# Swapping the packet sizes of two slabs between load and store in a 90-degree rotation

## Chip, cores and metric

The kernel runs on one core of one Trainium2 chip. The metric is the device time of one execution in microseconds (us), lower is better. Engines: DVE is VectorE, ACT is ScalarE, SP is SyncE, which here issues all transfers. The 16 DMA engines serve one queue.

## The reference

```python
def setup_inputs():
    batch, c, h, w = 32, 3, 256, 256
    return {"x": np.random.randn(batch, c, h, w).astype(np.float32)}

def reference(x):
    return np.rot90(x, k=-1, axes=(-2, -1)).astype(np.float32)
```

96 images of 256 x 256 floats are turned. Nothing is computed: 25.17 MB are read and 25.17 MB written.

## The kernel before

The images are cut into 12 slabs of 2 MB, numbered 0 to 11, and all 12 fit into SBUF at once. Every slab is loaded, turned by transposes on DVE, and stored. A row of the result is a column of the source, so each slab has one of two layouts on the way in and the other, or for pairs of slabs the same, on the way out:

- "short": a partition holds 8 image rows, one contiguous run and so one packet of 8 KB, for each half of the slab. One transfer of all 128 partitions for both halves (two for slab 0, one for each half).
- "long": a partition holds 16 image rows, one packet of 16 KB. Two transfers of 64 partitions each, on the even and on the odd ones.

```python
    RL, RS = 16, 8
    I = 2
    ...
    long_st = (0, 1, 2)          # loaded short, stored long
    both = (8, 10)
    paired = [n + a for n in both for a in range(2)]   # loaded long, stored long
    ...
    for n in (0, 1, 2, 3, 7, 4, 5, 6, *range(8, n_slabs)):
        if n in (1, 2):
            nc.sync.dma_start(out=fours(units[n]), in_=ld_short[n])
            continue
        for i in range(I):
            if n in long_st:
                ld = nc.sync.dma_start(out=fours(units[n])[:, i], in_=ld_short[n][:, i])
            else:
                ld = nc.sync.dma_start(out=units[n][i::I], in_=ld_long[n, i])
            if (n, i) == (last, 0):
                mark = ld

    home = [turned0] + units[:last]      # slab n is turned into the place of slab n - 1
    ...
    def store(n):
        if n in paired:
            ...
        elif n in long_st:
            for i in range(I):
                nc.sync.dma_start(out=st_long[n, i], in_=home[n][i::I])
        else:
            return nc.sync.dma_start(out=st_short[n], in_=fours(home[n]))

    for n in range(both[0]):
        turn(n)
    for n in (4, 3, 5, 6, 7, 1, 2):
        st = store(n)
        if n == 4:
            tc.add_manual_dep(st.ins, mark.ins.name, ...)   # stores after loads
    for n in range(both[0], n_slabs):
        turn(n)
        store(n)
    ...
    store(0)
```

`mark` makes the first store wait until the last load but one has landed. So all loads come first and all stores after them, in one queue that does not run empty.

## Time and profile before

| | before |
|---|---|
| device time, median of three runs | 123.28 us (123.15 to 123.40) |
| span of the profiled run | 121.5 us |
| bytes moved, packets of the queue | 50.33 MB, 97.9% of 16 engines' span |
| DVE busy | 90.6 us |
| loads done, stores done (last data packet) | 61.64 us, 120.30 us |

The page of the profile gives totals and the span in 40 slices. The view by stretches gives, for each stretch of time: its length, the busy time of DVE, ACT and POOL, the clock, the mean busy share of the 16 DMA engines, and GB/s. The trace also holds a record of every packet (start, duration, size); means and ends of packets in this text are from those. "Loads done" is where the records have moved half of the bytes. The lines themselves stand in the prediction.

### The profile page before, as it was taken

Reading aid. Unit: us, or ns where it says so; the run is one execution under the profiler, and the core shown is the slowest. Engines: PE = TensorE matmul, PEld = TensorE weight load, DVE = VectorE, ACT = ScalarE, POOL = GpSimd, SP = SyncE. Lnnn points to the kernel's source line nnn. Section 1 sums busy time; section 2 is a strip of 40 time slices with the busy share of each in tenths; the row PEclk is TensorE's granted clock in tenths of the full one; section 3 lists DMA queues with packets and bytes.
Section 4 is the critical chain, followed back from the end, with each engine's and each line's share of the span. In section 5 each row is a group of like instructions: output and inputs, shape, how many; then the busy total and the mean of one; then the engine's idle time right before and its main releaser. Section 6 shows DMA issues by size and latency. Waiting matters only on the chain.

```text
span 121.5 us, 134 instructions
## 1 busy us (share of the span) xinstructions
DVE 90.6 (75%) x24; ACT 4.9 (4%) x3; POOL 0.2 (0%) x4
## 2 busy tenths in 40 slices
DVE  0029999999999999999999999999999960000000
ACT  0000000000000000000040000000000038000000
POOL 0000000000000000000000000000000000000000
DMA  3999999999999999999999999999999999999994
GB/s 73 426 429 426 432 458 426 426 421 421 432 432 432 421 432 432 426 426 432 432 405 426 421 429 431 432 423 431 453 432 432 432 432 432 432 432 432 432 432 173
DMA packets 4752, 50.33 MB, mean 414 GB/s; under 512 B 656, under 2 KB 656, under 8 KB 656
## 3 DMA queue, kind: packets, MB, share of 16 engines
q1 hardware_dynamic: 4752, 50.33, 97.9%
HBM read 25.17 MB, written 25.17 MB: 414 GB/s over the span
## 4 chain that ended last, share of the span: by engine, by line
DVE 59%; issue 13%; DMA 6%; DVEq 3%; ACT 2%; ACTq 1%; SPq 0%
DVE u L116 53%; DVE turned L116 6%; DMA u<-in_x_dram 6%; DVEq L169 3%; ACT u L141 2%; ACTq L169 1%; SPq L92 0%; DVEq L116 0%
## 5 line engine op out<-in xcount | busy, mean ns | idle before, releaser
L116 DVE STREAM_TRANSPOSE u<-u 128x2048 f32<-128x2048 f32 x22 | 83.5, 3866 | 0.3
L116 DVE STREAM_TRANSPOSE turned<-u 128x2048 f32<-128x2048 f32 x2 | 7.1, 3586 | 8.2 <-DMA u<-in_x_dram 8.2
L141 ACT COPY u<-turned 128x2048 f32<-128x2048 f32 x2 | 3.6, 1869 | 35.6 <-DVE u L116 35.6
L141 ACT ACT_TABLE_LOAD x1 | 1.3, 1283 | 62.2 <-DMA u<-in_x_dram 62.2
L158 POOL MEMSET const-bfloat16-1.0<- 128x1 bf16 x1 | 0.1, 101 | 0.0
L158 POOL MEMSET const-uint8-127<- 128x1 uint8 x1 | 0.1, 101 | 0.0
L158 POOL MEMSET const-float32-0.0<- 128x1 f32 x1 | 0.1, 98 | 0.2 <-issue 0.2
L158 POOL MEMSET const-float32-1.0<- 128x1 f32 x1 | 0.1, 98 | 0.0
## 6 DMA issues: line engine op xcount, KB each, us to landing
u<-in_x_dram SPq DMA_DIRECT2D x20, 1024.0 KB, 19.6
out_dram<-u SPq DMA_DIRECT2D x14, 1024.0 KB, 15.6
out_dram<-u SPq DMA_DIRECT2D x5, 2048.0 KB, 16.0
u<-in_x_dram SPq DMA_DIRECT2D x2, 2048.0 KB, 13.7
```

The source lines that it names most:

```text
L116: nc.vector.transpose(out=dst[:, h * step : (h + 1) * step], in_=src[:, h * step : (h + 1) * step])
L141: nc.scalar.copy(out=fours(units[last])[:, i], in_=fours(turned0)[:, i])
L158: nc = _bacc.Bacc("TRN2", target_bir_lowering=False, num_devices=1)
L169: with _tile.TileContext(nc) as tc:
```

## The change

Slabs 1 and 2 change sides: loaded long (16 KB packets), stored short (8 KB packets). Their stores keep their place in the queue, behind those of slabs 4, 3, 5, 6 and 7, so that the stores of 8 KB packets lie together. The intent, as far as the edit shows it, is to load all but slab 0 with the larger packets.

```diff
-    long_st = (0, 1, 2)
+    long_st = (0,)
@@
-        if n in (1, 2):
+        if n in ():
             nc.sync.dma_start(out=fours(units[n]), in_=ld_short[n])
             continue
```

## The prediction

> **What bounds the kernel now.** I began with the page, for the total of the transfers. A kernel that only turns images by 90 degrees reads 25.17 MB and writes 25.17 MB, so the first question is whether the DMA engines ever rest.
>
> ```profile
> span 121.5 us, 134 instructions
> DVE 90.6 (75%) x24; ACT 4.9 (4%) x3; POOL 0.2 (0%) x4
> DMA  3999999999999999999999999999999999999994
> DMA packets 4752, 50.33 MB, mean 414 GB/s; under 512 B 656, under 2 KB 656, under 8 KB 656
> ...
> q1 hardware_dynamic: 4752, 50.33, 97.9%
> ```
>
> The DMA row is full from the second slice to the last but one, and the packets of the one queue fill 97.9% of 16 engines' span: 0.979 x 121.5 = 118.95 us of the 121.5. VectorE (DVE) has 90.6 us of work. The page's chain of waits nevertheless runs mostly through DVE:
>
> ```profile
> DVE 59%; issue 13%; DMA 6%; DVEq 3%; ACT 2%; ACTq 1%; SPq 0%
> DVE u L116 53%; DVE turned L116 6%; DMA u<-in_x_dram 6%; DVEq L169 3%; ACT u L141 2%; ACTq L169 1%; SPq L92 0%; DVEq L116 0%
> ```
>
> I do not take that chain for the bound. It follows instructions back and ends about 103 us into the span; after that only packets queued earlier drain, which no instruction stands for. The view by stretches decides. Its columns are the stretch in us, its length, busy time of DVE, ACT and POOL, clock, the mean busy share of the 16 DMA engines, and GB/s:
>
> ```profile
> 0.00:2.00 2.00, 0.00 (x0) 0.00 (x0) 0.20 (x4) 1.00 0.14 33
> 2.00:4.00 2.00, 0.00 (x0) 0.00 (x0) 0.00 (x0) 1.00 0.80 274
> 5.00:17.00 12.00, 8.74 (x3) 0.00 (x0) 0.00 (x0) 1.00 1.01 427
> 20.00:58.00 38.00, 37.83 (x10) 0.00 (x0) 0.00 (x0) 1.00 1.01 429
> 64.00:84.00 20.00, 19.97 (x6) 0.00 (x0) 0.00 (x0) 1.00 1.01 429
> 88.00:118.00 30.00, 11.13 (x4) 3.63 (x2) 0.00 (x0) 1.00 1.01 429
> ```
>
> I chose the four long stretches by kind of transfer: loads in 8 KB packets (slabs 0, 1, 2), loads in 16 KB packets (the rest), stores in 8 KB packets (slabs 4, 3, 5, 6, 7), stores in 16 KB packets (slabs 1, 2, 8 to 11, 0). All four move 427 to 429 GB/s with every engine busy. So the program is one queue of 50.33 MB: at 429 GB/s that is 117.3 us, plus the start (2.00 x 0.86 + 2.00 x 0.20 = 2.1 us lost in the first 4 us) and about 1.5 us after the last packet, 120.9 of the 121.5 us. The measured time, 123.28 us, is 1.8 us above the span, and I carry that over unchanged.
>
> **What the Trainium skill says.** "DMA: Bandwidth & Descriptors", section "Why small descriptors are slow (HBM only)", gives each packet a fixed overhead of about 3 cycles inside the engine, beside one cycle for every 32 bytes. For 8 KB that is 3 in 259 (1.2%), for 16 KB 3 in 515 (0.6%), so doubling the packet should save about 0.6% of a transfer. The trace agrees. Over the same four stretches its packet records have means of 310.0 ns (8 KB load), 614.1 ns (16 KB load), 309.0 ns (8 KB store) and 613.7 ns (16 KB store): two 8 KB packets cost 618 to 620 ns where one of 16 KB costs 614, 0.7 to 1%, the same in both directions. "SBUF — State Buffer", section "Door 1: The DMA port swizzle", warns that partitions 0 to 63 alone reach half of the ports; the 16 KB transfers here have 64 partitions too, but every second one of all 128, and their 429 GB/s shows that nothing is lost. The same page, "Who interferes with whom", says that transfers do not contend with the compute engines; the trace agrees: 429 GB/s with DVE fully busy (64 to 84 us) and also over 88 to 118 us, where it works 11 of 30 us.
>
> **The change part by part.** It moves slabs 1 and 2 from one group to the other.
> 1. Loads. Two issues of 2 MB, 512 packets of 8 KB, become four issues of 1 MB, 256 packets of 16 KB. Engine time 512 x 310.0 - 256 x 614.1 = 1.5 us less, over 16 engines 0.09 us less.
> 2. Stores. Four issues of 1 MB, 256 packets of 16 KB, become two of 2 MB, 512 packets of 8 KB. 512 x 309.0 - 256 x 613.7 = 1.1 us more, over 16 engines 0.07 us more.
> 3. Completion packets. There are 656 = 16 x 41 of them, for 41 transfers. Loads go from 22 to 24 and stores from 19 to 17: again 41, and 4096 data packets as before. Nothing gained or lost.
> 4. Sum on the path that sets the end: -0.02 us, that is, nothing. Each slab keeps one leg in each packet size; only the legs swap.
> 5. DVE. The order of instructions shows the same 24 transposes in the same order; four of them take the 16-rows-by-2 pattern in place of the 8-by-8 pattern with runs of 32 slots. The chain has the pair of slab 1 from 15.33 to 23.19 us (7.86), slab 2 to 31.03 (7.84), slab 3, which has the new pattern today, to 38.89 (7.86). No difference, and it lies beside the transfers anyway.
> 6. Arrival. DVE needs slab 1 at 15.33 and slab 2 at 23.19 us. In the records they land at 13.1 and 18.1 us. The bytes ahead of them in the queue stay the same, so they land within some tenths of that: 2 and 5 us of reserve.
> 7. Issue. SP keeps at most eight transfers open, since each waits for the one eight places before it. At the start those eight were 2 x 1 + 2 x 2 + 4 x 1 = 10 MB and become 8 MB, 20 us of work at 429 GB/s; the loads of 1 MB that run in this regime already take a median of 19.6 us from issue to landing with the engines at 1.01. In the stores the eight open ones now hold more bytes. Each 2 MB store is one issue of 0.4 to 0.9 us in place of two of about 1.4 us, so SP is free earlier, which is worth nothing while the queue is full.
>
> **Rivals.**
> - *The direction matters.* Writing to HBM in small packets could cost more than reading, so that the stores lose what the loads do not win back. For it: it is the only asymmetry in the change. Against it: 429 GB/s and 309 ns in 64 to 84 us, where exactly such stores run. Even 5% more on 4.19 MB (9.8 us) would be 0.5 us: 123.8.
> - *The queue runs dry at a hand-over.* The stores of slabs 8 and 9 wait for DVE at 84.73 us, those of 10 and 11 at 99.16. Against it: 14.7 MB of stores in front of slab 8 last from about 62 to 96 us, 11 us beyond its release; the 4.2 MB of slabs 8 and 9 then last to about 106, nearly 7 us beyond the second. One 2 MB store slot more or less in the ring of eight shifts what each issue waits for, but the slots waited for (stores of 3 to 7) are the oldest in the queue. A stall of one such transfer would cost at most 2 MB / 429 = 4.9 us: about 128.
> - *The start gets shorter.* Larger packets straight after slab 0 could fill the 16 engines sooner. Against it: slab 0 is still first in 8 KB packets, and its 16 packets on each engine cover the ramp, which is over by 4 us. At most some tenths: 123.0.
> - *DVE becomes the bound.* It would have to lose over 4 us (it ends at 99.2, the queue would be dry at about 106). Four instructions of unchanged length cannot do that.
>
> **Range and chances.** The sum leaves 123.28 - 0.02, so 123.26 us. Three runs of the kernel before spread from 123.15 to 123.4; the new one may also shift how the 16 engines finish relative to each other by up to half a 16 KB packet (0.3 us). I take 122.9 to 123.65. Two per cent are 2.5 us, over a hundred times the sum: faster by that 1%, slower by that 1% (only the dry queue would do it), the same 98%.
>
> **What would show it right or wrong.** Right: 4752 packets and 656 small ones again, about 98% of the queue's span, 427 to 429 GB/s in every stage, the first stretch now with 16 KB packets from about 8 us and the 8 KB stores lasting until about 96 us; mean transposes of 3.9 us; the first transpose still at 8.2 us. Wrong: a stretch of the DMA share below 0.95 between 4 and 118 us (a dry queue), a mean of 8 KB stores above 315 ns in 84 to 96 us (direction), or DVE waiting for a load at slab 1 or 2.

## The result, and the profile after

The changed kernel took 123.81 us in the median of six runs (123.68 to 124.01), against 123.30 us (123.15 to 123.40) for the kernel before. The ratio is 1.0044, 95% interval 1.0031 to 1.0057. A ratio here is the mean time of one kernel's fast runs over that of the other's of the same rounds, so it is not quite the ratio of the two medians. By the 2% rule that is "the same", but it is a real loss of half a microsecond, and it lies outside the predicted range.

The page of the changed kernel:

```profile
span 122.1 us, 134 instructions
DVE 90.4 (74%) x24; ACT 4.9 (4%) x3; POOL 0.2 (0%) x4
DMA  3999999999999999999999999999999999999993
DMA packets 4752, 50.33 MB, mean 412 GB/s; under 512 B 656, under 2 KB 656, under 8 KB 656
...
q1 hardware_dynamic: 4752, 50.33, 97.7%
...
DMA 51%; DVE 20%; issue 3%; DVEq 3%; SPq 3%; ACT 2%; ACTq 1%
```

Packets, bytes and the full DMA row are as predicted. The last line is the summary of the chain of waits. It now runs mainly over transfers where it ran over DVE before (59%), although neither kernel is bound by DVE: a reminder that this chain picks one of several ways that end close together.

The transposes, in the costliest groups (line, engine, operation, out and in, count, busy us, mean ns, idle before), of the kernel before:

```profile
L116 DVE STREAM_TRANSPOSE u<-u 128x2048 f32<-128x2048 f32 x22 | 83.5, 3866 | 0.3
```

and of the changed one:

```profile
L116 DVE STREAM_TRANSPOSE u<-u 128x2048 f32<-128x2048 f32 x22 | 83.4, 3848 | 0.3
```

DVE is not slower and waits no longer. The time must be in the queue. The view by stretches of the changed kernel, over the stretches of the prediction:

```profile
5.00:17.00 12.00, 8.80 (x3) 0.00 (x0) 0.00 (x0) 1.00 1.02 436
20.00:58.00 38.00, 37.83 (x10) 0.00 (x0) 0.00 (x0) 1.00 1.01 429
64.00:84.00 20.00, 19.96 (x6) 0.00 (x0) 0.00 (x0) 1.00 1.01 427
88.00:118.00 30.00, 10.91 (x4) 3.63 (x2) 0.00 (x0) 1.00 1.01 429
```

The early loads show 436 against 427 GB/s, the stretch of 8 KB stores 427 against 429. Both differences are too small to read from this view, which counts a packet whole where it starts: one 8 KB packet on each of 16 engines is 131 KB, which over 20 us is already 6.6 GB/s, and one 16 KB packet on each is 22 GB/s over 12 us. The very end tells more. The kernel before:

```profile
119.00:120.00 1.00, 0.00 (x0) 0.00 (x0) 0.00 (x0) 1.00 0.81 344
120.00:121.00 1.00, 0.00 (x0) 0.00 (x0) 0.00 (x0) 1.00 0.01 0
```

The changed one:

```profile
119.00:120.00 1.00, 0.00 (x0) 0.00 (x0) 0.00 (x0) 1.00 0.89 377
120.00:121.00 1.00, 0.00 (x0) 0.00 (x0) 0.00 (x0) 1.00 0.16 66
```

Before, all engines stop together shortly after 120 us. Afterwards some of them work on. The packet records give the sizes:

| | before | changed |
|---|---|---|
| first data packet starts | 1.76 us | 1.76 us |
| loads done | 61.64 us | 61.34 us |
| mean of 8 KB store packets, 63 to 76 us (slabs 4, 3, 5: not touched by the change) | 309.0 ns | 310.9 ns |
| share of those over 310 ns | 0% | 17% |
| mean of 8 KB store packets after 76 us | 309.1 ns | 311.8 ns |
| mean of 16 KB store packets after 99 us | 614.2 ns | 616.2 ns |
| mean end of the 16 engines' last packets | 120.21 us | 120.41 us |
| last of these ends | 120.30 us | 120.87 us |
| first to last of these ends | 0.14 us | 0.69 us |

"First to last" is called the end spread below. So the loads win 0.30 us, and the stores take 59.53 us where they took 58.66: 0.87 us lost. Of the net 0.57 us, 0.20 us is a later end in the mean over the engines, and 0.37 us is that the last engine ends further behind the mean. Stores are slow that are identical in both kernels.

The delay is not spread evenly. If each record is joined to the one whose end it meets, the queue falls into 16 strings of packets, presumably one for each engine (this joining is a reconstruction, not always unique; the records do not name the engine). A packet's record starts about 3 ns before the one ahead of it ends: 306 ns from start to start where each lasts 309, which is why the busy share can read 1.01. Durations in ns of consecutive 8 KB stores from 76 us on in the changed kernel, two strings of each sort, S being a completion packet:

```
S 309 309 309 309 309 309 309 309 309 309 309 309 309 309 309 309 S 309 309 309 ...
S 309 309 309 309 309 309 309 309 309 309 309 309 309 309 309 309 S 309 309 309 ...
S 315 318 313 314 316 316 312 313 319 312 313 314 314 316 312 314 S 318 316 312 ...
S 316 314 309 324 315 309 314 313 319 314 314 312 309 316 316 316 S 318 309 316 ...
```

Some strings run at exactly 309 ns for tens of microseconds, others have 309 to 324 ns and mostly over 310. The disturbance grows: in the changed kernel 11% of the 8 KB stores take over 310 ns from 63 to 66 us, 36% from 77 to 80, and 74% from 92 to 95. In the kernel before, every string between 63 and 66 us except for one packet reads 309 throughout.

### The profile page after: what moved, and what is told of

Its sections match the earlier page's. It is cut to its first block, busy times and chain, and to the rows that moved or that the text cites. A ratio compares the mean times of both kernels' runs of the same rounds, so it can differ in the third digit from the quotient of the medians.

```text
span 122.1 us, 134 instructions
## 1 busy us (share of the span) xinstructions
DVE 90.4 (74%) x24; ACT 4.9 (4%) x3; POOL 0.2 (0%) x4
## 4 chain that ended last, share of the span: by engine, by line
DMA 51%; DVE 20%; issue 3%; DVEq 3%; SPq 3%; ACT 2%; ACTq 1%
DMA u<-in_x_dram 45%; DVE u L116 20%; DMA out_dram<-u 6%; DVEq L169 3%; SPq L94 2%; ACT u L141 2%; ACTq L169 1%; SPq L92 1%; DVEq L116 0%; SPq L127 0%
```

## The experiments

Theory A: the changed loads leave the 16 engines in a relation to each other (their spacing in time) in which the stores then delay each other, changed or not. Theory B: the 8 KB stores of slabs 1 and 2 are what costs. Further rivals come up below: theory C is defined in the expectation of `split8`, D in that of `after_drain`, E in that of `before_nodve`. Each kernel ran beside the kernel before on the same chip; "8 KB stores" below is the mean of these packets from 63 to 76 us, which belong to slabs 4, 3 and 5, whose stores no experiment edits (from 64.5 us where the queue was emptied). These figures are of one profile for each run.

### The kernel before, again

No edit.

> The kernel before, unchanged, for a second profile and the noise of a run. All theories: ratio 1.000 within 0.001. If the spacing of the 16 engines in the queue is set by the program, the 8 KB stores between 64 and 84 us should again take a mean of 309.0 ns and the engines should finish the last transfer within 0.2 us of each other. If the spacing is a matter of luck in each run, this profile shows another spread.

123.32 us, ratio 1.0022 (0.9997 to 1.0046), not within the 0.001 expected: four of six runs took 123.16 to 123.32 us, but two took 123.99 and 124.03, longer than the median of the changed kernel. The profiled run is one of the four. In it the 8 KB stores had 309.5 ns and the end spread was 0.18 us, although the spread of the engines at the first landings was another one (0.71 us in place of 0.49). So that spread alone does not decide. But the program alone does not decide either: the kernel before can lose as much by itself. Of its other 55 runs none took over 123.65 us; no long run of it was profiled, so why two were long stays open.

### Only the loads

```diff
-        if n in (1, 2):
+        if n in ():
...
-            if n in long_st:
+            if n == 0:
                 ld = nc.sync.dma_start(out=fours(units[n])[:, i], in_=ld_short[n][:, i])
```

> Only the loads of slabs 1 and 2 take 16 KB packets; stores and transposes are those of the kernel before, so the result is wrong on purpose. Theory A (the loads set how the 16 engines are spaced in time, and that spacing later delays stores that the change never touched): the slowdown is here, 123.6 to 123.9 us, the unchanged 8 KB stores of slabs 4, 3, 5, 6, 7 at a mean above 310 ns, the last transfer finished over 0.5 us apart. Theory B (8 KB stores of slabs 1 and 2 are what costs): no slowdown, 123.0 to 123.3 us, 309.0 ns.

123.85 us, ratio 1.0045 (1.0033 to 1.0057): the whole loss. 8 KB stores 311.3 ns, 26% of them over 310, and the engines end 0.65 us apart. The result is wrong, as meant. Its last stretches:

```profile
119.00:120.00 1.00, 0.00 (x0) 0.00 (x0) 0.00 (x0) 1.00 0.88 377
120.00:121.00 1.00, 0.00 (x0) 0.00 (x0) 0.00 (x0) 1.00 0.12 49
```

Engines work past 120 us as in the changed kernel, although all its stores are those of the kernel before. This is the experiment that shows the cause as far as it is known: an edit of the loads alone slows stores that are the same.

### Only the stores

```diff
-        elif n in long_st:
+        elif n == 0:
             for i in range(I):
```

> Only the stores of slabs 1 and 2 take 8 KB packets; loads and transposes are those of the kernel before, so the result is wrong on purpose. Theory A: no slowdown, 123.2 to 123.4 us, 8 KB stores at 309.0 ns up to 96 us. Theory B: 123.6 to 123.9 us, with a mean above 311 ns between 84 and 96 us only.

123.43 us, ratio 1.0013 (1.0001 to 1.0025), end spread 0.20 us. 8 KB stores 309.0 ns up to 76 us, 309.9 ns after that, where the new ones lie. B is out as the cause of the half microsecond: these stores cost about 0.16 us, against 0.07 us predicted. Theory A's 123.2 to 123.4 us, with 309.0 ns throughout, was just missed too. The same two stretches:

```profile
119.00:120.00 1.00, 0.00 (x0) 0.00 (x0) 0.00 (x0) 1.00 1.23 524
120.00:121.00 1.00, 0.00 (x0) 0.00 (x0) 0.00 (x0) 1.00 0.01 0
```

### More transfers in the load queue, same packets

```diff
-        if n in (1, 2):
+        if n in ():
```

> The kernel before, with each 2 MB load of slabs 1 and 2 split into two of 1 MB, still in 8 KB packets; correct. Theory C (the number of transfers in the load queue, not the packet size, does it): 123.6 to 123.9 us. Theories A by packet size, and B: 123.2 to 123.4 us.

123.44 us, ratio 1.0012 (1.0000 to 1.0024), 8 KB stores 309.0 ns. The number of transfers (24 loads, as in the changed kernel) does not do it.

### Emptying the queue between loads and stores

Before and changed kernel, each with every store of the first loop waiting for the very last load:

```diff
-            if (n, i) == (last, 0):
+            if (n, i) == (last, I - 1):
...
-        st = store(n)
-        if n == 4:
+        for st in store(n):
             tc.add_manual_dep(st.ins, mark.ins.name, ...)
```

(`store` returns the list of its transfers for this.)

> The kernel before, but the first stores wait for the last load itself and not for the one before it, so that the queue runs empty at the hand-over and the 16 engines start the stores with a new spacing. Both theories: about 2 us slower than the kernel before, 125 to 126 us. Beside after_drain it gives the difference that is left when no spacing is handed over.

> The changed kernel with the same emptied queue at the hand-over. Theory A (the loads hand a bad spacing of the engines to the stores): the 0.5 us are gone or turned round, after_drain at most 0.15 us slower than before_drain, the same mean of the 8 KB stores within 0.5 ns. Rival D (the changed kernel's stores are slow for a reason of their own, whatever the spacing): after_drain still 0.4 to 0.7 us slower.

Both took 125.66 us, with ratios of 1.0193 (1.0176 to 1.0210) and 1.0194 (1.0179 to 1.0209). The gap at the hand-over and the stores behind it, from the kernel before with the emptied queue:

```profile
61.00:64.00 3.00, 2.96 (x2) 1.28 (x1) 0.00 (x0) 1.00 0.36 142
64.00:84.00 20.00, 19.96 (x6) 0.00 (x0) 0.00 (x0) 1.00 1.01 419
```

and the changed one:

```profile
61.00:64.00 3.00, 2.97 (x2) 1.28 (x1) 0.00 (x0) 1.00 0.43 175
64.00:84.00 20.00, 19.96 (x6) 0.00 (x0) 0.00 (x0) 1.00 1.01 419
```

The difference between the kernels is gone, which speaks against D; `loads_only`, where the slow stores are those of the kernel before, had already shown that the stores need no reason of their own. It fits something that passes through the hand-over while the queue stays full. It does not prove it: the emptied queue slows the stores of both kernels (317.4 and 318.3 ns, so the expected agreement within 0.5 ns was missed), and that could hide a difference. What I had not expected is that a fresh start of the stores is worse than either: about 70% of the packets over 310 ns. Yet here the engines end only 0.17 and 0.19 us apart. Slow stores and an uneven end are two things, and the one can come without the other.

### Without VectorE

Both kernels without transposes and copies:

```diff
-        for h in range(parts):
+        for h in range(0):
             nc.vector.transpose(...)
...
-    for i in range(I):
-        nc.scalar.copy(out=fours(units[last])[:, i], in_=fours(turned0)[:, i])
-    home[0] = units[last]
```

(`home[0]` is the last slab's place from the start.)

> The kernel before without its transposes and its two copies (wrong result on purpose); the same transfers in the same order. Theory E (VectorE's reading and writing of SBUF delays packets of the queue, and so spreads the engines): 16 KB loads at 611 ns flat in place of 614, loads done 0.2 us or more earlier. If VectorE has no part in it: 614 ns as before, 123.1 to 123.4 us.

> The changed kernel without transposes and copies (wrong result on purpose). Theory E: the slowdown goes away with VectorE, within 0.2 us of before_nodve, 8 KB stores at 309 ns. Theory A without VectorE: still 0.4 to 0.7 us slower than before_nodve, with 8 KB stores above 310 ns.

123.13 us (0.9987, 0.9972 to 1.0002) and 123.60 us (1.0022, 1.0007 to 1.0037), so 0.47 us between their medians. 8 KB stores 309.0 and 311.1 ns. The 16 KB loads between 28 and 46 us take 614 ns with DVE and without it. Theory E is out: VectorE has no part in it, which agrees with the Trainium skill's "SBUF — State Buffer", section "Who interferes with whom".

### A small extra transfer ahead of the stores

Into the kernel before and the changed one:

```diff
+    extra = extra_pool.tile([8, 1024], fp32, name="extra")
+    nc.sync.dma_start(out=extra, in_=rows_in[0:32].rearrange("(p r) w -> p (r w)", r=4))
```

> The kernel before with one extra transfer of 32 KB (8 partitions of 4 KB, never used) at the end of the loads, so that about half of the 16 engines enter the stores some 155 ns later in relation to the others; result correct. The work itself is about 0.1 us on the engines concerned. Theory A (spacing between engines decides): the stores that ran at 309.0 ns now exceed 310 ns in the mean, 123.6 to 124.0 us. If something else than spacing is handed over: 309.0 ns still, 123.3 to 123.5 us.

> The changed kernel with the same extra transfer; correct. Theory A: the mean of the 8 KB stores changes, in whichever direction, by over 0.5 ns against the 311 ns of the changed kernel, and may heal it (123.3 to 123.5 us). If something else than spacing is handed over: 311 to 312 ns and 123.9 to 124.0 us.

123.48 us (1.0026, 1.0010 to 1.0041) with 8 KB stores still at 309.0 ns, and 123.97 us (1.0059, 1.0046 to 1.0071) with 311.3 ns. The eight extra packets took 159 to 166 ns each, and up to six or seven were in flight at once, so presumably eight engines were set back by that much against the others. In the profiled runs it broke nothing in the one and healed nothing in the other (two of the six runs of the first, unprofiled, took 123.70 and 123.86 us). This speaks against A in its simple form: this shift, of half of the engines by half a packet, did not matter.

The same for all 16 engines, in the changed kernel, with a tile of 16 partitions:

```diff
+    extra = extra_pool.tile([16, 1024], fp32, name="extra")
+    nc.sync.dma_start(out=extra, in_=rows_in[0:64].rearrange("(p r) w -> p (r w)", r=4))
```

> The changed kernel with one extra transfer of 64 KB (16 partitions of 4 KB, never used) at the end of the loads: one more packet on each of the 16 engines, so the spacing between them is kept and only where the stores stand in each engine's list moves. Correct. If the spacing matters: still slow, 123.9 to 124.1 us, 8 KB stores above 310.5 ns. If the place in the list matters (the changed kernel enters the stores after exactly 128 entries on each engine, 104 of data and 24 of completion): healed, 309.0 ns, 123.3 to 123.5 us.

123.94 us, ratio 1.0053 (1.0040 to 1.0067), engines ending 0.92 us apart. The 8 KB stores had 309.9 ns, milder than the 310.5 expected and close to the 309.5 of the kernel before in its second profile, but the loss is all there: here it is mostly the uneven end, with a mean end of 120.30 us and a last one of 121.07. A place in the list that two entries more would change (one of data, one of completion on each engine) is out; larger shifts were not tried.

### How many slabs, and which

Correct kernels: only slab 2 changed, or only slab 1, or slabs 0 and 7 loaded short (and stored long) with all others but the paired ones the other way round.

```diff
-    long_st = (0, 1, 2)
+    long_st = (0, 1)        # one_slab;  (0, 2) in slabs02;  (0, 7) in slab7
-        if n in (1, 2):
+        if n in (1,):       # one_slab;  (2,) in slabs02;  (7,) in slab7
```

> Only slab 2 changed (loaded with 16 KB, stored with 8 KB packets), slab 1 as before; correct. If the cost is a share per slab: 123.5 us. If it is a matter of which spacing comes out: either 123.2 to 123.4 or 123.7 to 123.9 us, not between.

123.30 us, ratio 1.0004 (0.9990 to 1.0017), 8 KB stores 309.0 ns. This half of the change costs nothing that can be measured.

> Slab 1 changed (16 KB loads, 8 KB stores), slab 2 as before; correct. The twin of one_slab with the other slab. If one more slab in 8 KB loads is enough to keep the stores undisturbed, whichever it is: 309.0 ns in 64 to 84 us, 123.2 to 123.4 us. If it has to be slab 1: 311 ns and 123.7 to 123.9 us.

123.55 us, ratio 1.0024 (1.0012 to 1.0037). 8 KB stores 309.0 ns up to 76 us as expected, then 310.5 ns, and the time lies between both expectations. This other half costs about 0.30 us (0.0024 x 123.27), half of the whole loss. So the times do not rule out a share for each slab, if the shares may differ; against it stand the first stores, undisturbed in both halves.

> Slabs 0 and 7 in 8 KB loads and 16 KB stores, all others the other way round; correct. Slab 7 is the fifth in the queue of loads, late enough to meet the loads that no longer run at 611 ns. By the same pattern: 8 KB stores at 309.0 ns from 64 us, 123.2 to 123.5 us, not faster than the kernel before. If the place of the extra slab matters: slow as the changed kernel, 123.7 to 123.9 us.

123.67 us (123.37 to 123.96), ratio 1.0034 (1.0017 to 1.0050). 309.2 ns from 63 to 76 us, as the pattern wants; but the 8 KB stores after that take 311.1 ns in the mean (311.8 behind the 16 KB stores of slab 7), and the time was a miss.

Wrong on purpose, with the stores of the kernel before: 8 KB loads for slabs 0, 10 and 11 (late8), for 0 and 11 (last11), and for none at all (all16).

```diff
-        if n in (1, 2):
+        if n in (10, 11):             # late8, with mark set at slab 10; () in last11 and all16
...
-            if n in long_st:
+            if n == 0:                # late8; (0, last) in last11; () in all16
```

> 8 KB loads for slab 0 and for the last two slabs (10, 11) in place of 1 and 2; stores and transposes as before, so wrong on purpose. If the last loads before the hand-over set the spacing: 8 KB stores at 309.0 ns and the early 16 KB loads at 611 ns, 122.9 to 123.2 us, faster than before. If the first loads set it: 311 ns and 123.7 to 123.9 us as with the change.

123.45 us, ratio 1.0012 (1.0000 to 1.0024). All 8 KB stores at 309.0 ns and the 16 KB ones after 99 us at 611.0. But the late 8 KB loads themselves were slow (314.1 ns in the mean from 54 to 60 us), the engines ended 0.57 us apart, and the 122.9 to 123.2 us expected with undisturbed stores were missed. So undisturbed stores alone do not make the time; an uneven end costs too.

> As loads_only, but the very last slab (11) also loaded in 8 KB packets; wrong on purpose. If the packets just ahead of the hand-over count: 309.0 ns in 66 to 84 us and 123.2 to 123.5 us. If only early 8 KB loads count: 311 ns and 123.7 to 123.9 us.

123.43 us, ratio 1.0007 (0.9995 to 1.0020), 8 KB stores 309.0 ns.

> loads_only taken one step further: slab 0 too is loaded with 16 KB packets, so no load has 8 KB; stores and transposes as before, wrong on purpose. By the pattern of the runs so far (slow stores wherever slab 0 is the only one loaded in 8 KB packets, undisturbed ones wherever one more slab is) this one has to be slow: 123.7 to 124.0 us, the unchanged 8 KB stores above 310 ns. If it runs at 309.0 ns and 123.0 to 123.3 us, the pattern is not about how many 8 KB loads there are.

124.27 us, ratio 1.0078 (1.0065 to 1.0090), 8 KB stores 312.8 ns, 40% over 310. Slower than the expected range; the first packets also start later (2.08 us against 1.76), which may be why. The pattern held where it could have failed.

### The changed kernel, again

> The changed kernel itself, for a second profile. If the slow stores belong to the program and not to the luck of one run: 123.7 to 124.0 us, 8 KB stores at a mean of 310.5 ns or more between 64 and 84 us, the last transfer finished over 0.5 us apart on the 16 engines. If to luck: other values than in the first profile of it.

123.71 us (123.48 to 124.03), ratio 1.0036 (1.0018 to 1.0053). 8 KB stores 312.0 ns, engines ending 0.69 us apart. Two of the four runs (123.48 and 123.54) are below the expected 123.7, but in the profiled run (123.88) stores and spread are as in the first profile: the loss comes back, though not in full in every run.

### All profiles together

| kernel | slabs in 8 KB loads | 8 KB stores, 63 to 76 us (ns) | end spread (us) | last packet ends (us) | median (us) |
|---|---|---|---|---|---|
| before | 0, 1, 2 | 309.0 | 0.14 | 120.30 | 123.28 |
| before, again | 0, 1, 2 | 309.5 | 0.18 | 120.32 | 123.32 |
| split8 | 0, 1, 2 | 309.0 | 0.22 | 120.31 | 123.44 |
| only the stores | 0, 1, 2 | 309.0 | 0.20 | 120.49 | 123.43 |
| before, nudged | 0, 1, 2 | 309.0 | 0.25 | 120.36 | 123.48 |
| before, no VectorE | 0, 1, 2 | 309.0 | 0.19 | 120.21 | 123.13 |
| one_slab | 0, 1 | 309.0 | 0.19 | 120.28 | 123.30 |
| slabs02 | 0, 2 | 309.0 | 0.46 | 120.47 | 123.55 |
| slab7 | 0, 7 | 309.2 | 0.49 | 120.57 | 123.67 |
| last11 | 0, 11 | 309.0 | 0.29 | 120.22 | 123.43 |
| late8 | 0, 10, 11 | 309.0 | 0.57 | 120.48 | 123.45 |
| changed | 0 | 310.9 | 0.69 | 120.87 | 123.81 |
| changed, again | 0 | 312.0 | 0.69 | 120.89 | 123.71 |
| only the loads | 0 | 311.3 | 0.65 | 120.73 | 123.85 |
| changed, no VectorE | 0 | 311.1 | 0.76 | 120.84 | 123.60 |
| changed, nudged | 0 | 311.3 | 0.65 | 120.85 | 123.97 |
| changed, padded | 0 | 309.9 | 0.92 | 121.07 | 123.94 |
| all16 | none | 312.8 | 0.65 | 121.11 | 124.27 |

Among the kernels with a full queue the profiles fall into two groups: at least one slab besides slab 0 in 8 KB loads, wherever it stands among the loads, and the first stores run at 309.0 to 309.5 ns; no such slab, and they take 309.9 to 312.8 ns with the engines ending 0.65 us or more apart. The line is narrow (309.5 against 309.9, where two profiles of the changed kernel differ by 1.1), and it holds for the first stores only. In other kernels the disturbance begins later: over 310 ns are 3% of the 8 KB stores of slabs02 from 77 to 80 us and 37% from 86 to 89, 13% and 38% of those of slab7, and 17% in the second profile of the kernel before from 82 to 85. As far as these profiles show, the changed loads do not switch it on; they bring it forward to the first stores. In time, too, slab7 (1.0034) cannot be told from the changed kernel run again (1.0036). No experiment came out clearly faster than the kernel before and correct, so there is no better version to show.

## Why the prediction was wrong

- What bounds the kernel: right. Packets, bytes and the queue's 98% came as stated, and DVE without any work at all changed little.
- Step 1, the loads, 0.09 us less: the sign was right, the size too small. They were done 0.30 us earlier. The mean of 614.1 ns was taken over 20 to 58 us, but the early 16 KB loads of the changed kernel run at 611.0 ns, and the 8 KB loads that they replaced had partly been slow (311.3 ns in the mean from 12 to 18 us). About 0.1 us of it is there already when the first transfer of slab 0 completes, which is the same in both kernels (5.02 against 5.12 us in the mean over the engines; 5.05 in the second profile of the kernel before).
- Step 2, the stores, 0.07 us more: about right for the changed stores alone (0.16 us, interval 0.01 to 0.31, from the ratio times 123.26 us).
- Readings slightly off, without weight for the sum: after the last data packet 1.2 us pass (120.30 of 121.5), not 1.5; 16 KB stores from 88 to 118 us have 613.6 ns, not 613.7; and as records of consecutive packets overlap by 3 to 4 ns, steps 1 and 2 are each overstated by about 0.04 us, with opposite signs.
- Step 4, the sum of -0.02 us, is the step that failed. It adds up only the packets that change their size and lets all others keep their duration. The loads alone cost 0.55 us (0.0045 x 123.26), through stores that nobody edited: 309.0 to 311.3 ns, and an uneven end. "Each slab keeps one leg in each packet size; only the legs swap" is true of the counts and false of the time, because in these runs a store's packet does not have a fixed duration: it changed with the loads that ran before it.
- Steps 3, 5, 6 and 7 held: 656 completion packets, transposes of 3.85 us against 3.87, the first transpose at 8.2 us, no wait of DVE, no gap in the queue.
- The rivals: the queue running dry, DVE as the bound and the quicker start were rightly set aside. "The direction matters" named the right size (0.5 us, 123.8) by luck: its 8 KB stores of slabs 1 and 2 are not the cause. No rival had the loads slowing down other slabs' stores.
- The range allowed 0.3 us for how the engines finish relative to each other; the end spread went from 0.14 to 0.69 us, and the mean moved by 0.20 us on top.
- "Wrong" was to show as a mean above 315 ns; it showed as 312.3 ns there. The mark was set too wide for a case in which 2 ns on every packet of 8 KB stores are 0.2 us.

What stays open: what the loads hand over, and what in them does it. It is not the number of transfers, a shift of the list by two entries, VectorE's traffic, or a shift of half of the engines by 160 ns. Two rivals were not separated from the packet size. A slab in 16 KB packets also has another form of transfer, on every second partition in place of all. And the kernels without a second slab in 8 KB loads are also those with the fewest load packets, 96 to 105 for each engine against 112 or more in all others; a run with 16 KB loads and many small extra packets could tell. That it is a relation between particular engines is what the reconstructed strings suggest, but no run shows it: the records do not name the engines, and the one experiment that moved engines against each other changed nothing.

## What to carry to other kernels

In a kernel whose queue is always full, do not add up only the packets that a change touches: take the durations of all stages again, and look at how far apart the engines end, since the last one sets the time. Test a change that moves two things by making each alone; here a load-side edit that speeds the loads up cost its time a stage later, and only the half-changed kernels showed it. Look at single runs and not only at the median: two of six runs of the unchanged kernel were as long as the changed one. Where the expected sum is near zero, a range as narrow as the scatter of the old kernel's runs is too narrow: half a per cent can come from packets that the change does not touch.

## What the Trainium skill lacked or had wrong

- "DMA: Bandwidth & Descriptors", section "Why small descriptors are slow (HBM only)": a fixed overhead per packet fits the undisturbed durations (a line through the 309 ns of 8 KB and the 611 ns of 16 KB gives 158 ns for 4 KB, and the shortest extra packet took 159). The prediction's estimate from the page, 0.6% saved by doubling the packet, is of the right size: two undisturbed 8 KB packets take 618 ns where one of 16 KB takes 611, 1.1%, or 0.8% from start to start (2 x 305.9 against 607.1 ns). But the page has nothing on packets of the same kind and direction taking 309.0 or 310 to 313 ns, for tens of microseconds, depending on what was loaded earlier in the queue.
- The same page, section "Anatomy of one DMA — SWDGE (gpsimd) path", gives about 2 us of fixed cost for a transfer on that path. The runs, with transfers issued by SP, show a similar size: in the kernel before with the emptied queue, 1.7 us lie between the last loads and the first stores (mean over the engines, 61.46 to 63.17 us), out of 2.4 us lost in all (125.66 against 123.28). The rest is what the page does not say: the stores behind the restart are slower, 317 to 318 ns for 8 KB from 64.5 to 76 us.
- No page gives a figure for how far apart the 16 engines of one queue end a balanced list of transfers: here it was 0.14 to 0.92 us, and that alone was 0.37 of the 0.57 us.
